# Memory keys with the contraction outermost, first loads on two queues, memory norm summed by slab, fewer stores, in a one-core decoder trunk

## The chip, the cores and the metric

The kernel runs on one core of one Trainium2 chip. The metric is the device time of one execution in microseconds, lower is better. All times below come from executions on the chip.

## The reference, cut to what matters

Two layers (`DEPTH = 2`) are run on a prompt of 256 tokens and on 8 samples of 4 tokens, with shared weights, `D_MODEL = 1024`, all in float32. Each layer begins with keys and values of 256 memory tokens; they depend on the memory input alone, so the kernel computes those of both layers before anything else. The trunk ends in one norm.

```python
def rmsnorm(x, g):
    xf = x.astype(F32)
    y = xf * lax.rsqrt(jnp.mean(xf * xf, axis=-1, keepdims=True) + EPS)
    return (y * g.astype(F32)).astype(x.dtype)
...
        mem_h = rmsnorm(mem_prompt, mem_norm[i])
        mk = (mem_h @ w_mem_k[i]).reshape(bp, n_mem, MEM_HEADS, MEM_HEAD_DIM)
        mv = (mem_h @ w_mem_v[i]).reshape(bp, n_mem, MEM_HEADS, MEM_HEAD_DIM)
        xp, npool, nconv, nssm = trunk_layer(
...
    y_prompt = rmsnorm(xp, final_norm)
    y_sample = rmsnorm(xs, final_norm)
```

## The kernel before

**Weights.** All weights are cut into tiles of 128 x 128 and packed in the order of use, eight to a slab of 512 KB. `Stream` runs them past TensorE. A slab is loaded by SyncE's queue into one of four `raw` buffers, then split into two float32r parts, `whi` on ScalarE (line 139) and `wlo = raw - whi` on VectorE (line 148). The first slab is loaded and split in two halves. Each product is three matmuls: high weight by high activation, high by low, low by high.

**Order of the work.** Every engine runs its instructions in program order. `take` hands out weight tiles; at the first tile of slab `s` it calls `tick(s)`, which issues loads up to slab `s+5`, then one stage of every generator that was given to `W.start(gen, delay)`, then the splits up to `whi(s+3)` and `wlo(s+2)`. A load into a `raw` buffer waits for the `wlo` that reads the buffer's last slab.

**The head.** The memory input `mem` lies transposed, contraction (1024) on partitions in eight chunks, two to a tile, 256 tokens wide. `mem_split` (from line 435) makes `memh` on ScalarE and `meml` on VectorE of a chunk. Slabs 0 to 3 are the keys of layer 0, 4 to 7 its values, 8 to 11 and 12 to 15 those of layer 1; the feed-forward starts at slab 16. In the keys one slab is one head: the eight chunks of the contraction go into one PSUM bank, then the next head starts. The values keep the contraction outermost already: a slab is two chunks, and two banks (`ps_v0`, `ps_v1`) take them.

The memory norm is applied behind the products. `mem_norm` squares the eight chunks on ScalarE, adds them into `macc` on GpSimd (`square`, line 297), sums columns with two small matmuls (`ps_mem`), takes the inverse root into `rv`, and spreads it over partitions with two more (`ps_rm`) into `Rm`. `mem_out` multiplies the key banks by `Rm` and stores them, `mem_out_v` the value banks by `rv`. `first_norm` prepares the first feed-forward's input chunk by chunk, and `load_x` loads it.

**The tail.** `Final.add` squares each of the eight chunks of `x` as the last down-projection delivers it and adds it into `facc` on GpSimd, the last chunk on VectorE. `Final.finish` sums columns (`ps_fin`), takes the inverse root, spreads it over partitions (`ps_spread`), copies that to `Rf`, and multiplies and stores each chunk by itself.

Of the kernel before, what the change touches and what calls it, by code (L numbers as in the profile page):

```python
# [20 lines left out]
NM = 256  # L21
# [23 lines left out]
def group_order(tiles, cuts):  # L45
    """Weight tiles (tile, k) of a group of products: all tiles up to each cut of k in turn."""
    for a, b in zip((0,) + cuts[:-1], cuts):
        for t in tiles:
            for k in range(a, b):
                yield t, k  # L50
# [41 lines left out]
def weight_plan():  # L92
    plan = []
    for i in range(L):
        for h in range(4):
            plan += [("w_mem_k", i, k * P, h * P) for k in range(KC)]
        for k in range(KC):
            plan += [("w_mem_v", i, k * P, c * P) for c in range(4)]
# [8 lines left out]
class Stream:  # L107
    """Runs the packed weight tiles past TensorE, each split into two float32r parts.

    Every SLAB tiles make a tick: the split of a later slab is issued, then one stage  # L110
    of every piece of side work that is under way."""
# [77 lines left out]
def trunk_kernel(ctx, tc, wpack, xT, memT, vecs, consts, wdt, wpool, hpool, hconv, h0T, kT, vC,  # L189
# [31 lines left out]
    def blocks(name):  # L221
        """Two tiles of zeros for block_fill()."""
# [5 lines left out]
    def block_fill(us, srcs, copy):  # L228
        """Block b of 32 columns, of each of the four slices, gets the slice's samples with all but sample b zero."""
# [60 lines left out]
    def products(tiles, cuts, xs):  # L290
        """One PSUM bank per tile: W[:, cols].T @ x."""
# [13 lines left out]
    def rstd_cols(accs, starts, width, name):  # L305
        """1 / sqrt(mean + eps) of the column sums of accs, tokens on partitions: [128, len(accs) * len(starts)]."""
# [16 lines left out]
    def rstd_rows(r, t, sums, width):  # L323
        """r = 1 / sqrt(sums / width + eps), elementwise; stages."""
# [11 lines left out]
    def spread(r):  # L336
        """out[p, t] = r of token t, for every partition p; r holds tokens 0.., 128.., 160.. by column."""
# [6 lines left out]
    class Norm:  # L344
        """Collects sum(x^2) chunk by chunk and splits x * gain for the products."""
# [23 lines left out]
    class Final:  # L369
        """The last norm: x * gain in place, then its scale and the output."""  # L370
# [4 lines left out]
        def add(self, c):  # L375
            xc = x[:, c, :]
            if c < KC - 1:
                square(self.acc, xc, c == 0)
            else:
                sq = tmp("sqr")  # L380
                tt(sq, xc, xc, ALU.mult)
                tt(self.acc, self.acc, sq, ALU.add)
            act(xc, xc, AF.Copy, scale=vec[:, V_FIN + c:V_FIN + c + 1])

        def add_lo(self, c):
            pass

        def finish(self):
            r = rstd_cols([self.acc], TOK, D, "fin")
            R = rp.tile([P, T], F32, tag="R", name="Rf")  # L390
            act(R, spread(r)[:, :T], AF.Copy)
            for c in (0, 5, 1, 2, 6, 3, 4, 7):
                tt(x[:, c, :], x[:, c, :], R, ALU.mult, G if c in (5, 6) else V)
                nc.sync.dma_start(out=o_y[:, c, :], in_=x[:, c, :])
# [17 lines left out]
    mem = [unit(f"mem{j}") for j in range(KC // 2)]  # L412

    def load_mem(j):
        nc.sync.dma_start(out=mem[j][:, :, :NM], in_=memT[:, 2 * j:2 * j + 2, :])

    gain0 = cp.tile([P, KC], F32, name="gain0")
    load_mem(0)
    nc.sync.dma_start(out=gain0, in_=vecs[:, V_MEM:V_MEM + KC])
    W.load_to(0)  # L420
    for j in range(1, KC // 2):
        load_mem(j)
    W.load_to(1)
    nc.sync.dma_start(out=vec, in_=vecs)
    W.load_to(2)
    nc.sync.dma_start(out=con, in_=consts)
    W.load_to(3)
# [18 lines left out]
    def mem_norm():  # L446
        for c in range(KC):
            square(macc, chunk(mem, c)[:, :NM], c == 0)
        yield
        yield  # L450
# [3 lines left out]
        yield  # L454
# [21 lines left out]
    def mem_out(i, kps, h, ksb):  # L476
        yield
# [11 lines left out]
    warm = rp.tile([P, 1], F32, tag="warm", name="warm", bufs=1)  # L489
    G.memset(warm, 0.0)  # L490
    act(warm, warm, AF.Copy)
    mem_split(0, range(2))
    W.split_to(0, 0)
    mem_split(0, range(2, KC))
    W.split_to(1, 1)
    W.start(mem_norm())
    W.start(load_x(), 1)
    n0 = Norm("n0", lambda c: col(0, V_F1, c))
    for i in range(L):
        mh, ml = mhl[i]  # L500
        ksb = k4.tile([P, 4, NM], F32, tag="k4", name="ksb")
        for h in range(4):
            ps = bank("ps_k")
            ws = [W.take() for k in range(KC)]
            for k in range(KC):
                mm(ps[:, :NM], ws[k][0], chunk(mh, k)[:, :NM], k == 0, False)
                mm(ps[:, :NM], ws[k][0], chunk(ml, k)[:, :NM], False, False)
            for k in range(KC):
                mm(ps[:, :NM], ws[k][1], chunk(mh, k)[:, :NM], False, k == KC - 1)
            W.start(mem_out(i, ps, h, ksb), max(0, 5 - h) if i == 0 else 0)  # L510
        if i == 0:
            W.start(first_norm(n0))
# [51 lines left out]
    def mixer(i, cur, nxt):  # L564
# [65 lines left out]
        def dt_work(ps_dt):  # L630
# [19 lines left out]
            # log1p(e) = 2 atanh(e / (2 + e))  # L650
# [13 lines left out]
            # cumulative sums, heads on partitions and tokens on partitions; sums to the end of the group  # L664
# [149 lines left out]
        def heads4(g):  # L814
            """Four heads of the prompt's scan: two pairs of heads, one group of B and C."""
# [170 lines left out]
        def softmax(ps, n):  # L986
            """Rows of ps [128, n, 256] (scores) to weights; stages."""
# [354 lines left out]
```

## Time and profile before

| | |
|---|---|
| median of 3 runs | 1600.78 us (1600.12 to 1602.69) |
| span of the profiled execution (first to last instruction) | 1597.1 us |
| that execution's own time | not recorded; the median is 3.7 us above the span |
| TensorE busy (PE, matmul) | 1558.0 us, 98% of the span |
| VectorE (DVE) / ScalarE (ACT) / GpSimd (POOL) busy | 67% / 50% / 19% |
| memory traffic over the span | 173 GB/s |
| chain that ended last, TensorE's share | 87% |

PE is TensorE's matmul row, PEld its weight loads, SPq the DMA issues of SyncE. Where a row says `[2.31 <-DVE meml L246]` the engine stood idle for 2.31 us before that instruction, and VectorE's writing of `meml` at line 246 ended it. The names before `<-` are outputs, those behind it inputs.

### The profile page before, as it was taken

To read this page: it belongs to the slowest core of one execution; us is meant where nothing else is said; L and a number is where in the kernel's file an instruction comes from. 1 tells how busy PE (TensorE), PEld (TensorE's weight loads), DVE (VectorE), ACT (ScalarE), POOL (GpSimd) and SP (SyncE) were. 2 spreads that over 40 slices of the span, in tenths; PEclk is the share of its full clock that TensorE was granted. 3 is DMA by queue.
4 is the path that set the end of the run, shared out by engine and by line. 5 is a ranking of instruction groups with operands and counts; after the bars stand their busy time and mean duration, and the time that the engine had idled before them with its cause. 6 is when DMAs were issued, how large, how long until landed. Compare 5 with 4: busy or idle time off the path is not lost.

```text
span 1597.1 us, 29305 instructions
## 1 busy us (share of the span) xinstructions
PE 1558.0 (98%) x11792; PEld 1502.7 (94%) x11792; DVE 1066.3 (67%) x1598; ACT 804.0 (50%) x1231; POOL 302.9 (19%) x368
## 2 busy tenths in 40 slices
PE   7999999988999999999999999999999999999997
PEld 6899999887889999999999999988888999999997
DVE  6765645788777867656456665588778786766643
ACT  7444434465565546444445444456557454644442
POOL 3000001368233102000000000046823320200001
PEclk9999999999999999999999999999999999999999
DMA  6744444546465454444444444554655545444452
GB/s 244 230 167 166 164 165 171 196 147 233 168 212 193 147 173 167 162 165 166 165 166 160 171 161 169 178 185 151 238 170 188 203 159 169 158 168 167 159 171 70
DMA packets 81287, 278.00 MB, mean 174 GB/s; under 512 B 9088, under 2 KB 14336, under 8 KB 81152
## 3 DMA queue, kind: packets, MB, share of 16 engines
q1 hardware_dynamic: 81152, 276.14, 50.2%
q8 instruction: 92, 1.51, 0.4%
q14 instruction: 43, 0.35, 0.1%
HBM read 262.39 MB, written 13.71 MB: 173 GB/s over the span
## 4 chain that ended last, share of the span: by engine, by line
PE 87%; DVE 8%; ACT 2%; DMA 1%; POOL 1%; issue 1%; SPq 0%; DVEq 0%; ACTq 0%; POOLq 0%
PE ps L249 61%; PE pd L249 18%; DVE cacc L246 4%; PE ps_y L249 2%; PE ps_v L249 1%; PE ps_k L249 1%; ACT L252 1%; DMA raw<-wpack 1%; PE ps_up L249 1%; DVE wlo L148 1%; DVE cbuf L237 1%; ACT cacc L252 1%; PE ps_yo L249 1%; ACT whi L139 1%; PE ps_sp L249 0%
## 5 line engine op out<-in xcount | busy, mean ns | idle before, releaser
L148 DVE TENSOR_TENSOR wlo<-raw,whi 128x1024 fp32r<-128x1024 f32 (+1 forms) x409 | 517.8, 1267 | 266.8 <-ACT hidh L252 99.9
L139 ACT ACTIVATE whi<-raw 128x1024 fp32r<-128x1024 f32 (+1 forms) x441 | 463.7, 1054 | 329.3 <-PE ps L249 153.2
L249 PE MATMUL ps<-n1h,whi 128*128 128x288 f32 x896 | 274.4, 306 | 5.4 <-DVE Bst L237 5.4
L249 PE MATMUL ps<-n1h,wlo 128*128 128x288 f32 x896 | 266.9, 298 | 4.8 <-POOL wlo L148 4.8
L249 PE MATMUL ps<-n1l,whi 128*128 128x288 f32 x896 | 266.3, 297 | 0.0
L249 PE MATMUL ps<-n2h,whi 128*128 128x288 f32 x704 | 208.8, 297 | 0.0
L249 PE MATMUL ps<-n0h,whi 128*128 128x288 f32 x704 | 208.6, 296 | 0.0
L249 PE MATMUL pd<-hidh,whi 128*128 128x288 f32 x704 | 208.4, 296 | 0.0
L249 PE MATMUL ps<-n0l,whi 128*128 128x288 f32 x704 | 207.7, 295 | 0.0
L249 PE MATMUL pd<-hidl,whi 128*128 128x288 f32 x704 | 207.7, 295 | 0.0
L249 PE MATMUL ps<-n2l,whi 128*128 128x288 f32 x704 | 207.7, 295 | 0.0
L249 PE MATMUL ps<-n2h,wlo 128*128 128x288 f32 x704 | 207.0, 294 | 0.0
L249 PE MATMUL ps<-n0h,wlo 128*128 128x288 f32 x704 | 207.0, 294 | 0.0
L249 PE MATMUL pd<-hidh,wlo 128*128 128x288 f32 x704 | 207.0, 294 | 0.0
L237 POOL TENSOR_TENSOR acc<-acc,sqr 128x288 f32<-128x288 f32 x42 | 44.7, 1064 | 786.9 <-ACT sqr L252 785.9
L249 PEld LDWEIGHTS ps<-n1h,whi 128*128 128x128 f32 x896 | 170.3, 190 | 16.1 <-DVE Bst L237 5.8
L249 PEld LDWEIGHTS ps<-n1h,wlo 128*128 128x128 f32 x896 | 170.4, 190 | 7.3 <-POOL wlo L148 6.9
L249 PEld LDWEIGHTS ps<-n1l,whi 128*128 128x128 f32 x896 | 170.5, 190 | 0.7
L249 PEld LDWEIGHTS ps<-n0h,wlo 128*128 128x128 f32 x704 | 132.6, 188 | 0.0
L249 PEld LDWEIGHTS pd<-hidh,wlo 128*128 128x128 f32 x704 | 132.6, 188 | 0.0
L249 PEld LDWEIGHTS ps<-n2h,wlo 128*128 128x128 f32 x704 | 132.6, 188 | 0.0
L249 PEld LDWEIGHTS ps<-n2l,whi 128*128 128x128 f32 x704 | 132.1, 188 | 0.1
(297 smaller groups left out, 2877.5 us busy)
## 6 DMA issues: line engine op xcount, KB each, us to landing
raw<-wpack SPq DMA_DIRECT2D x439, 512.0 KB, 3.3
kb<-kT SPq DMA_DIRECT2D x16, 512.0 KB, 5.1
vb<-vC SPq DMA_DIRECT2D x16, 512.0 KB, 4.6
hb<-h0T SPq DMA_DIRECT2D x16, 512.0 KB, 5.8
o_ssm_s<-hb SPq DMA_DIRECT2D x16, 512.0 KB, 5.0
x<-xT SPq DMA_DIRECT2D x4, 288.0 KB, 4.1
o_y<-x SPq DMA_DIRECT2D x8, 144.0 KB, 1.8
mem<-memT SPq DMA_DIRECT2D x4, 256.0 KB, 4.6
```

The lines of the kernel that those rows point to most:

```text
L139: nc.scalar.activation(out=hi[:, a], in_=self.loaded[self.n_hi][:, a], func=AF.Copy)
L148: eng.tensor_tensor(out=lo[:, a], in0=raw[:, a], in1=self.his[n][:, a].bitcast(F32), op=ALU.subtract)
L237: (eng or V).tensor_tensor(out=out, in0=a, in1=b, op=op)
L246: V.scalar_tensor_tensor(out=out, in0=a, scalar=s, in1=b, op0=op0, op1=op1)
L249: PE.matmul(out, lhsT=lhsT, rhs=rhs, start=start, stop=stop)
L252: A.activation(out=out, in_=a, func=func, **kw)
```

## The change

Keys: the packed order of `w_mem_k` becomes that of `w_mem_v`, so a key slab is two chunks of the contraction for all four heads, and four PSUM banks are filled side by side. Loads: `mem` 0 and the gain go to ScalarE's queue; on SyncE's the two halves of slab 0 come first, then `mem` 1, slab 1, `mem` 2 and 3, slab 2, `vec`, slab 3, `con`. Splits: `meml`/`memh` of chunks 4 to 7 come after the split of slab 1. Memory norm: the seven additions go from GpSimd to VectorE, and the eight squares are put into two ticks (1 and 2) in place of one (0). The start of `load_x` is 2 ticks later, that of `first_norm` 3 ticks. Two matmuls on a tile of zeros (`still`) are put ahead of everything on TensorE; nothing reads their result.

Tail: the last chunk's square is no longer added into `facc`; its column sums are taken by themselves and added at [128, 3]. A dummy square root stands behind chunk 5. The chunks are multiplied straight from the PSUM bank on VectorE (six) and from `Rf` on GpSimd (two), and stored by five DMAs, three of them for two chunks.

```diff
@@ def weight_plan():
-        for h in range(4):
-            plan += [("w_mem_k", i, k * P, h * P) for k in range(KC)]
-        for k in range(KC):
-            plan += [("w_mem_v", i, k * P, c * P) for c in range(4)]
+        for name in ("w_mem_k", "w_mem_v"):
+            for k in range(KC):
+                plan += [(name, i, k * P, c * P) for c in range(4)]
@@ class Final
-                sq = tmp("sqr")
-                tt(sq, xc, xc, ALU.mult)
-                tt(self.acc, self.acc, sq, ALU.add)
+                self.sq = tmp("sqr")
+                tt(self.sq, xc, xc, ALU.mult)
             act(xc, xc, AF.Copy, scale=vec[:, V_FIN + c:V_FIN + c + 1])
+            if c == KC - 3:
+                act(warm, warm, AF.Sqrt)
...
+        def sums(self, acc):
+            ps = bank("ps_fin")
+            for j, s in enumerate(TOK):
+                mm(ps[:, j:j + 1], acc[:, s:s + P], ones[:, 0:1])
+            return ps
+
         def finish(self):
-            r = rstd_cols([self.acc], TOK, D, "fin")
+            v, r = (sp.tile([P, 3], F32, tag=f"fin{k}", name=f"fin{k}") for k in range(2))
+            ts(v, self.sums(self.acc)[:, :3], 1.0 / D, ALU.mult, EPS, ALU.add)
+            stt(v, self.sums(self.sq)[:, :3], 1.0 / D, v, ALU.mult, ALU.add)
+            act(r, v, AF.Sqrt)
...
+            ps = spread(r)
             R = rp.tile([P, T], F32, tag="R", name="Rf")
-            act(R, spread(r)[:, :T], AF.Copy)
-            for c in (0, 5, 1, 2, 6, 3, 4, 7):
-                tt(x[:, c, :], x[:, c, :], R, ALU.mult, G if c in (5, 6) else V)
-                nc.sync.dma_start(out=o_y[:, c, :], in_=x[:, c, :])
+            act(R, ps[:, :T], AF.Copy)
+            for c, n in ((0, 0), (6, 0), (1, 2), (2, 0), (3, 2), (7, 2), (4, 1), (5, 1)):
+                if c < 6:
+                    tt(x[:, c, :], ps[:, :T], x[:, c, :], ALU.mult)
+                else:
+                    tt(x[:, c, :], x[:, c, :], R, ALU.mult, G)
+                if n:
+                    nc.sync.dma_start(out=o_y[:, c + 1 - n:c + 1, :], in_=x[:, c + 1 - n:c + 1, :])
@@ first loads
-    load_mem(0)
-    nc.sync.dma_start(out=gain0, in_=vecs[:, V_MEM:V_MEM + KC])
+    load_mem(0, A)
+    A.dma_start(out=gain0, in_=vecs[:, V_MEM:V_MEM + KC])
     W.load_to(0)
-    for j in range(1, KC // 2):
-        load_mem(j)
+    load_mem(1, nc.sync)
     W.load_to(1)
+    for j in range(2, KC // 2):
+        load_mem(j, nc.sync)
+    W.load_to(2)
     nc.sync.dma_start(out=vec, in_=vecs)
-    W.load_to(2)
+    W.load_to(3)
     nc.sync.dma_start(out=con, in_=consts)
-    W.load_to(3)
@@ def mem_norm():
-            square(macc, chunk(mem, c)[:, :NM], c == 0)
-        yield
-        yield
+            src = chunk(mem, c)[:, :NM]
+            if c == 0:
+                act(macc, src, AF.Square)
+            else:
+                sq = tmp("sqr", NM)
+                act(sq, src, AF.Square)
+                tt(macc, macc, sq, ALU.add)
+            if c % 4 == 3:
+                yield
         yield
         r = rstd_cols([macc], (0, P), D, "mem")
@@ head
+    still = wide("still")
+    V.memset(still, 0.0)
...
+    ps = bank("ps_still")
+    for j in range(2):
+        mm(ps, still[:, :P], still)
     mem_split(0, range(2))
     W.split_to(0, 0)
-    mem_split(0, range(2, KC))
+    mem_split(0, range(2, 4))
     W.split_to(1, 1)
-    W.start(mem_norm())
-    W.start(load_x(), 1)
+    mem_split(0, range(4, KC))
+    W.start(mem_norm(), 1)
+    W.start(load_x(), 3)
...
+        pss = [bank("ps_k") for h in range(4)]
+        for k in range(KC):
+            ws = [W.take() for h in range(4)]
+            for part, xs in ((0, mh), (0, ml), (1, mh)):
+                for h in range(4):
+                    mm(pss[h][:, :NM], ws[h][part], chunk(xs, k)[:, :NM], k == 0 and part == 0 and xs is mh,
+                       k == KC - 1 and part == 1)
         for h in range(4):
-            ps = bank("ps_k")
-            ws = [W.take() for k in range(KC)]
-            for k in range(KC):
-                mm(ps[:, :NM], ws[k][0], chunk(mh, k)[:, :NM], k == 0, False)
-                mm(ps[:, :NM], ws[k][0], chunk(ml, k)[:, :NM], False, False)
-            for k in range(KC):
-                mm(ps[:, :NM], ws[k][1], chunk(mh, k)[:, :NM], False, k == KC - 1)
-            W.start(mem_out(i, ps, h, ksb), max(0, 5 - h) if i == 0 else 0)
+            W.start(mem_out(i, pss[h], h, ksb), 1 if i == 0 else 0)
         if i == 0:
-            W.start(first_norm(n0))
+            W.start(first_norm(n0), 3)
```

How the instructions stand is told by three places. The first is TensorE at the start of layer 0's keys. Before, from the end of the first head into the second (`memh0` holds chunks 0 and 1, `memh3` chunks 6 and 7):

```order
L249 MATMUL ps_k_167<-memh3_125,whi_134 128x256
L249 MATMUL ps_k_167<-meml3_129,whi_134 128x256
L249 MATMUL ps_k_167<-memh0_122,wlo_137 128x256 x2
L249 MATMUL ps_k_167<-memh1_123,wlo_137 128x256 x2
L249 MATMUL ps_k_167<-memh2_124,wlo_137 128x256 x2
L249 MATMUL ps_k_167<-memh3_125,wlo_137 128x256 x2
L249 MATMUL ps_k_224<-memh0_122,whi_152 128x256
L249 MATMUL ps_k_224<-meml0_126,whi_152 128x256
```

Of the change, TensorE's first key matmuls (`whi_139` is slab 0):

```order
L248 MATMUL ps_k_172<-memh0_127,whi_139 128x256
L248 MATMUL ps_k_173<-memh0_127,whi_139 128x256
L248 MATMUL ps_k_174<-memh0_127,whi_139 128x256
L248 MATMUL ps_k_175<-memh0_127,whi_139 128x256
L248 MATMUL ps_k_172<-meml0_131,whi_139 128x256
L248 MATMUL ps_k_173<-meml0_131,whi_139 128x256
L248 MATMUL ps_k_174<-meml0_131,whi_139 128x256
L248 MATMUL ps_k_175<-meml0_131,whi_139 128x256
L248 MATMUL ps_k_172<-memh0_127,wlo_142 128x256
```

Before, the first slab uses all eight memory chunks and its low part comes last; now it uses chunks 0 and 1 alone, and its low part from the ninth matmul on.

The second place is VectorE between the memory splits and the norm's root. Before (`wlo_154` is slab 1, `wlo_230` slab 3, `wlo_262` slab 4):

```order
L246 SCALAR_TENSOR_TENSOR meml3_129<-mem3_96,gain0_97,memh3_125 128x256 x2
L148 TENSOR_TENSOR wlo_154<-raw_106,whi_152 128x1024
L148 TENSOR_TENSOR wlo_198<-raw_109,whi_194 128x1024
L148 TENSOR_TENSOR wlo_230<-raw_112,whi_196 128x1024
L148 TENSOR_TENSOR wlo_262<-raw_168,whi_228 128x1024
L243 TENSOR_SCALAR rs_v_294<-ps_mem_291 128x2
```

Of the change (`wlo_184` is slab 2, `wlo_224` slab 3, `wlo_266` and `wlo_297` slabs 4 and 5):

```order
L245 SCALAR_TENSOR_TENSOR meml3_134<-mem3_96,gain0_97,memh3_130 128x256 x2
L147 TENSOR_TENSOR wlo_184<-raw_108,whi_180 128x1024
L236 TENSOR_TENSOR macc_118<-macc_118,sqr_213 128x256
L236 TENSOR_TENSOR macc_118<-macc_118,sqr_216 128x256
L236 TENSOR_TENSOR macc_118<-macc_118,sqr_219 128x256
L147 TENSOR_TENSOR wlo_224<-raw_111,whi_182 128x1024
L236 TENSOR_TENSOR macc_118<-macc_118,sqr_252 128x256
L236 TENSOR_TENSOR macc_118<-macc_118,sqr_255 128x256
L236 TENSOR_TENSOR macc_118<-macc_118,sqr_258 128x256
L236 TENSOR_TENSOR macc_118<-macc_118,sqr_261 128x256
L147 TENSOR_TENSOR wlo_266<-raw_176,whi_222 128x1024
L147 TENSOR_TENSOR wlo_297<-raw_178,whi_264 128x1024
```

The seven additions into `macc` now stand on VectorE, three ahead of slab 3's low part and four ahead of slab 4's.

The third place is VectorE behind the last chunk's square, to the end. Before:

```order
L237 TENSOR_TENSOR sqr<-x 128x288
L237 TENSOR_TENSOR facc<-facc,sqr 128x288
L243 TENSOR_SCALAR rs_v<-ps_fin 128x3
L317 RECIPROCAL rs_r<-rs_r 128x3
L246 SCALAR_TENSOR_TENSOR rs_v<-rs_v,rs_r 128x3
L237 TENSOR_TENSOR rs_v<-rs_v,rs_r 128x3
L246 SCALAR_TENSOR_TENSOR rs_r<-rs_v,rs_r 128x3
L237 TENSOR_TENSOR x<-x,Rf 128x288 x6
```

Of the change:

```order
L236 TENSOR_TENSOR sqr<-x 128x288
L242 TENSOR_SCALAR fin_17868<-ps_fin 128x3
L245 SCALAR_TENSOR_TENSOR fin_17868<-ps_fin,fin_17868 128x3
L399 RECIPROCAL fin_17869<-fin_17869 128x3
L245 SCALAR_TENSOR_TENSOR fin_17868<-fin_17868,fin_17869 128x3
L236 TENSOR_TENSOR fin_17868<-fin_17868,fin_17869 128x3
L245 SCALAR_TENSOR_TENSOR fin_17869<-fin_17868,fin_17869 128x3
L236 TENSOR_TENSOR x<-ps_spread,x 128x288 x6
```

The 128 x 288 addition is gone, one operation at 128 x 3 is new, and the six products read the PSUM bank in place of `Rf`.

## Rows read from the trace of the kernel before

**Rows 1.** The page, busy time and share of the span by engine.

```profile
PE 1558.0 (98%) x11792; PEld 1502.7 (94%) x11792; DVE 1066.3 (67%) x1598; ACT 804.0 (50%) x1231; POOL 302.9 (19%) x368
```

**Rows 2.** TensorE's waits, whole run: total us, times, longest us.

```profile
PE ps_mem L249 <- POOL macc L237: 2.5, 1, 2.5
PE ps_k L249 <- DVE meml L246: 2.3, 1, 2.3
```

**Rows 3.** Busy time, granted clock and traffic by stretch, us from the start.

```profile
core 0: us, PE busy (x) PEld busy (x) DVE busy (x) ACT busy (x) POOL busy (x), PEclk, DMA share, GB/s
0.00:5.76 5.76, 0.00 (x1) 0.00 (x1) 0.91 (x3) 3.02 (x5) 0.30 (x5) 1.00 0.58 184
5.76:10.84 5.08, 4.67 (x14) 3.44 (x15) 3.90 (x8) 3.36 (x8) 0.00 (x0) 1.00 0.91 307
10.84:14.26 3.42, 3.42 (x22) 3.42 (x23) 1.34 (x2) 3.42 (x10) 1.60 (x2) 1.00 1.04 423
21.36:26.01 4.65, 4.65 (x29) 4.65 (x29) 2.54 (x8) 3.33 (x7) 0.00 (x0) 0.69 0.82 265
63.62:1584.93 1521.31, 1503.66 (x11482) 1454.61 (x11481) 1015.73 (x1521) 762.67 (x1159) 286.01 (x347) 1.00 0.50 172
1584.93:1597.10 12.17, 1.68 (x12) 1.49 (x12) 5.69 (x14) 2.43 (x4) 2.03 (x2) 0.70 0.27 97
```

**Rows 4.** Timeline of the start: start us, duration us, instruction, idle before.

```profile
0.74 0.44 SPq L415 DMA_DIRECT2D mem<-memT  x1
1.74 0.90 SPq L130 DMA_DIRECT2D raw<-wpack  x2
3.68 0.91 ACT L252 ACTIVATE memh<-mem,gain 128x256 fp32r<-128x256 f32 x2 [1.45 <-DMA gain<-vecs]
...
5.08 1.38 ACT L139 ACTIVATE whi<-raw 128x512 fp32r<-128x512 f32 x2 [0.49 <-DMA raw<-wpack]
...
5.76 0.58 PE L249 MATMUL ps_k<-memh,whi 128*128 128x256 f32 x1 [5.76 <-ACT whi L139]
...
10.84 1.06 ACT L139 ACTIVATE whi<-raw 128x1024 fp32r<-128x1024 f32 x1 [0.40 <-DMA raw<-wpack]
```

**Rows 5.** Timeline, TensorE: eight key matmuls back to back, twice.

```profile
14.94 1.11 PE L249 MATMUL ps_k<-memh,wlo 128*128 128x256 f32 x8
...
24.30 1.91 PE L249 MATMUL ps_k<-memh,wlo 128*128 128x256 f32 x8
```

**Rows 6.** The chain that ended last: start us, us, what.

```profile
54.80 0.48 PE ps_norm L249 x2
55.28 8.33 PE ps_v L249 x36
```

**Rows 7.** Timeline of the memory norm, and one VectorE split.

```profile
12.11 2.25 ACT L252 ACTIVATE sqr<-mem 128x256 f32<-128x256 f32 x7
12.59 8.72 POOL L237 TENSOR_TENSOR macc<-macc,sqr 128x256 f32<-128x256 f32 x7 [11.75 <-ACT sqr L252]
...
23.30 1.22 DVE L148 TENSOR_TENSOR wlo<-raw,whi 128x1024 fp32r<-128x1024 f32 x1
```

**Rows 8.** Timeline of the tail.

```profile
1586.01 0.46 DVE L237 TENSOR_TENSOR facc<-facc,sqr 128x288 f32<-128x288 f32 x1
1586.49 1.28 ACT L252 ACT_TABLE_LOAD   x1
1586.52 0.83 PE L249 MATMUL ps_fin<-con,facc 128*128 128x1 f32 x6 [1.61 <-DVE facc L237]
...
1587.79 0.20 ACT L252 ACTIVATE rs_r<-rs_v 128x3 f32<-128x3 f32 x1
...
1589.73 0.41 ACT L252 ACTIVATE Rf<-ps_spread 128x288 f32<-128x288 f32 x1 [1.74 <-PE ps_spread L249]
1590.17 3.49 DVE L237 TENSOR_TENSOR x<-x,Rf 128x288 f32<-128x288 f32 x6 [1.39 <-ACT Rf L252]
...
1590.66 4.23 SPq L394 DMA_DIRECT2D o_y<-x  x8
```

More of the change, by code (lines that the diff above doesn't have):

```diff
@@ L379, in add @@
             else:
-                sq = tmp("sqr")
-                tt(sq, xc, xc, ALU.mult)
-                tt(self.acc, self.acc, sq, ALU.add)
+                self.sq = tmp("sqr")
+                tt(self.sq, xc, xc, ALU.mult)
             act(xc, xc, AF.Copy, scale=vec[:, V_FIN + c:V_FIN + c + 1])
+            if c == KC - 3:
+                act(warm, warm, AF.Sqrt)
         def add_lo(self, c):
             pass
-        def finish(self):
-            r = rstd_cols([self.acc], TOK, D, "fin")
-            R = rp.tile([P, T], F32, tag="R", name="Rf")
-            act(R, spread(r)[:, :T], AF.Copy)
-            for c in (0, 5, 1, 2, 6, 3, 4, 7):
-                tt(x[:, c, :], x[:, c, :], R, ALU.mult, G if c in (5, 6) else V)
-                nc.sync.dma_start(out=o_y[:, c, :], in_=x[:, c, :])
+        def sums(self, acc):
[3 more added lines that the diff above has]
+            return ps
+        def finish(self):
+            v, r = (sp.tile([P, 3], F32, tag=f"fin{k}", name=f"fin{k}") for k in range(2))
+            ts(v, self.sums(self.acc)[:, :3], 1.0 / D, ALU.mult, EPS, ALU.add)
+            stt(v, self.sums(self.sq)[:, :3], 1.0 / D, v, ALU.mult, ALU.add)
+            act(r, v, AF.Sqrt)
+            V.reciprocal(out=r, in_=r)
+            stt(v, v, -0.5, r, ALU.mult, ALU.mult)
+            tt(v, v, r, ALU.mult)
+            stt(r, v, 1.5, r, ALU.add, ALU.mult)
+            ps = spread(r)
+            R = rp.tile([P, T], F32, tag="R", name="Rf")
+            act(R, ps[:, :T], AF.Copy)
[6 more added lines that the diff above has]
+                    nc.sync.dma_start(out=o_y[:, c + 1 - n:c + 1, :], in_=x[:, c + 1 - n:c + 1, :])
             yield
@@ L412, in trunk_kernel, with load_mem @@
     mem = [unit(f"mem{j}") for j in range(KC // 2)]
-    def load_mem(j):
-        nc.sync.dma_start(out=mem[j][:, :, :NM], in_=memT[:, 2 * j:2 * j + 2, :])
+    def load_mem(j, eng):
+        eng.dma_start(out=mem[j][:, :, :NM], in_=memT[:, 2 * j:2 * j + 2, :])
     gain0 = cp.tile([P, KC], F32, name="gain0")
-    load_mem(0)
-    nc.sync.dma_start(out=gain0, in_=vecs[:, V_MEM:V_MEM + KC])
+    load_mem(0, A)
+    A.dma_start(out=gain0, in_=vecs[:, V_MEM:V_MEM + KC])
     W.load_to(0)
-    for j in range(1, KC // 2):
-        load_mem(j)
+    load_mem(1, nc.sync)
     W.load_to(1)
+    for j in range(2, KC // 2):
+        load_mem(j, nc.sync)
+    W.load_to(2)
     nc.sync.dma_start(out=vec, in_=vecs)
-    W.load_to(2)
+    W.load_to(3)
     nc.sync.dma_start(out=con, in_=consts)
-    W.load_to(3)
     Rm = tmp("Rm", NM)
@@ L453, in mem_norm @@
         V.tensor_copy(out=rv, in_=r)
-        yield
         yield
@@ L476, in mem_out @@
     def mem_out(i, kps, h, ksb):
-        yield
         tt(ksb[:, h, :], kps[:, :NM], Rm, ALU.mult)
```

## The prediction

> **What bounds the kernel now.** I read the page first: TensorE is busy 98% of the span [rows 1]. Then the stretches: from 63.62 to 1584.93 us, where the feed-forwards and mixers run, it is busy 1503.66 of 1521.31 us at full granted clock [rows 3]. The change touches nothing there, so I take those 1521.3 us as they are. What is left is the head up to 63.62 us and the tail of 12.17 us [rows 3]. The sum is a sum of shifts: how much earlier the first feed-forward starts, and how much shorter the tail is.
>
> In the head the reader should see four losses. TensorE starts at 5.76 us, when the first half of slab 0 is split [rows 4]. It first runs slowly: eight key matmuls take 1.91 us at the lower of the two clock levels (1.2 GHz) and 1.11 us at the upper (2.4 GHz), which the granted clock of 0.69 over 21.36 to 26.01 shows as a mixture [rows 3, 5]. It waits 2.5 us for the sum of squares, which GpSimd adds up for 8.72 us, and 2.3 us for `meml` of layer 1 [rows 2, 7]. The values of layer 0 start at 26.01 us, the edge of a stretch [rows 3].
>
> **The change part by part, head.** A key matmul has 256 columns, 0.213 us each at 1.2 GHz; eight of them and an overhang of 0.2 behind the last make the slow row's 1.91. Read the same way, the fast row gives (1.11 - 0.17) / 8 = 0.118 us each [rows 5]. So a slab of 24 is 2.8 us fast, 5.1 slow; the four key slabs 11.3 or 20.4. A value slab of 12 is 8.33/3 = 2.8 us fast [rows 6].
>
> *First product.* ScalarE waited for the gain until 3.68, then split `mem` 0 (0.91), then waited for slab 0's half until 5.08 [rows 4]. The change issues the slab's first half at the front of its own queue, one 0.44 us issue and the gain's sooner [rows 4], so that wait of 0.49 can go. Against it: `mem` 0 now shares the DMA engines with slab 0. Bounds: 5.3 us (the 0.49 saved) and 6.8 us (`mem` 0 usable only when slab 0's first half was, 5.08, then 0.91 and two half splits of 0.69); I take 6.0, nearer to the middle since neither row shows two queues.
>
> *Data.* Up to 5.76 us 184 GB/s moved 1.06 MB, up to 10.84 another 307 x 5.08 = 1.56 MB, then 423 GB/s [rows 3]. Before, slab 1 was the 2.10th MB in the queue's order; by these rates it had moved at 9.15, and it was usable at 10.84 [rows 4], a lag of 1.7 us. In the new order slab 1 is complete at 1.57 MB (usable 9.1), slab 2 at 2.62 MB (12.5), slab 3 at 3.34 MB with `vec` (14.2). This is the point of the reordering: a key slab now needs only its own two chunks, so TensorE can follow the loads.
>
> *Splits and slab 3.* ScalarE splits slab 3 from 14.2 to 15.3 (1.06 each, [rows 4]); then four squares at 0.32 (2.25/7, [rows 7]) end at 16.6. VectorE has three additions into `macc` queued ahead of slab 3's low part. I price one at 0.46, the same addition at 288 columns [rows 8]; the first starts when the second square is there (16.0), so they end at 17.4, and `wlo` of slab 3 (1.22, [rows 7]) at 18.6. That is the added wait: behind these additions stand VectorE's splits, and TensorE waits for them. On TensorE slabs 0 to 2 are through by about 16 at the fast rate; of slab 3 the eight high products can go, the other 16 (1.9 us) wait for 18.6 and end at 20.5. The column sums `ps_mem` cost some 0.6 (two columns; three took 0.83 at the end [rows 8]). **The values start at 21.1 in place of 26.0: 4.9 us.** The wait on GpSimd goes with it: the last four additions end at 18.6 + 4 x 0.46 = 20.4, before TensorE asks. If the additions cost nothing, slab 3 ends at 19 and the values start at 19.6; if TensorE is slow through slabs 0 and 1 (to 16.2) it costs nothing more, since slab 3 waits anyway; slow through slab 2 it costs 1 to 2 us.
>
> *The zero matmuls* are two of 512 columns in float32. `ps_norm`, the same kind at 288 columns, took 0.48 [rows 6], so each is 0.85 us fast or 1.7 slow, 3.4 together; begun near 1.3 us they end before 5. They cost nothing while the first product is later than that; without this cover they cost up to 3.4. What they bring is a clock that may have risen earlier, which slab 3's wait hides.
>
> A rule of the Trainium skill, page "TensorE: Matmul & The Clock Gate", section "Part 1: The HAM clock gate", says that the clock is throttled by default, that activity releases it, and that the monitor does not restart with the kernel, so the number of slow matmuls varies from run to run. No row here shows work ahead of 5.76 us, so it can't be held against the trace; if the rise came only after slab 2, the values would start 1 to 2 us later, which is a rival below.
>
> *From the values to the feed-forward* it was 63.62 - 26.01 = 37.6 us. The wait of 2.3 us for `meml` [rows 2] came since VectorE had to make all eight chunks of layer 1 before the first head was done; now two chunks are needed per slab, and `first_norm` with its GpSimd additions begins three ticks later. I take the whole 2.3 as gone, bounds 0 and 2.5. What is late next is `rv`: slabs 4 and 5's low parts stand ahead of it on VectorE (20.4 + 2 x 1.22 = 22.8), then a root and five small operations, each near the 0.20 of the tail's root [rows 8], 1.2 in all: 24.0, and `ps_rm` is asked for at 21.1 + 2.8 = 23.9. I add 0.2, bounds 0 and 1.5. **Feed-forward at 21.1 + 37.6 - 2.3 + 0.2 = 56.6 us in place of 63.62: 7.0 us.** `first_norm` ends three ticks (some 8 us) later against the feed-forward; its result is wanted four slabs into it, some 11 us or more, so this is hidden by those products; uncovered it would cost the part over 8.
>
> A second rule, page "DMA: Bandwidth & Descriptors", section "Queues, rings and completion order": each DMA engine takes turns between the queues it has work for, packet by packet. No run here shows two queues. By it `mem` 0, in pieces half as long as slab 0's, would land only with slab 0's second half, and the first product would come near the 6.8 of my bounds; slab 3's wait hides that in the sum.
>
> **The tail.** Gone from the path: the addition into `facc`, 0.46, with its hand-over 0.55; the table load's excess, since the root started at 1587.79 although `ps_fin` ended at 1587.35 and its scaling is a small operation of some 0.2, so 0.2; the copy `Rf`, 0.44 from 1589.73 to 1590.17 [rows 8]. New: one 128 x 3 operation is the same length as the one it replaces on the path. So the products start 1.2 us earlier. They last 3.49 us now, with eight stores issued over 4.23 [rows 8]; the last issue begins some 0.8 us after the last product. Five issues need 5 x 0.45 = 2.2 us, so the last store follows its product at once: 0.8 more at best, 0.2 at worst if two-chunk stores land later or the products from PSUM are slower. **Tail: 1.4 to 2.1, taken as 1.9.** The dummy root puts 1.3 us on ScalarE some 15 us before the end; there it is busy 50% [rows 1], so it is hidden.
>
> **Sum.** 7.0 + 1.9 = 8.9 us. The span becomes 1588.2 from 1597.1; the median of the runs is 3.7 above the span and I leave that difference: 1600.8 - 8.9 = **1591.9 us**. Differences of up to 0.2% (3.2 us) can hardly be told from no change here.
>
> **Rivals.**
> - *Follows the loads.* The additions don't hold slab 3 (squares earlier or VectorE faster): values at 19.6, `ps_rm` without a wait: 1.7 us better, 1590.2; with the tail at 2.1 and faster loads 1588.5. For it: VectorE's idle time between slabs. Against: program order.
> - *The head gives back.* VectorE takes splits, `meml`, `ksb` and `macc` in less time than before and again is late in layer 1's keys: the 2.3 us stay and `ps_rm` waits 1.2: 1591.9 + 3.3 = 1595.2.
> - *Clock late.* All four key slabs slow: 6.0 + 20.4 + 0.9 = 27.3 for the values, 6.2 later than forecast: 1598.1; slow through slab 2 only: 1593.5. For it: before, the rows from 5.76 on are slow for about 7 us, with gaps. Against: now the engine has fewer gaps when slow.
> - *Slower.* The same clock mechanism, kept low through the values of layer 0 as well, because the load-paced keys leave gaps: 48 value matmuls at twice 0.23 add 11 us to the 1598.1: 1609. It decides once the slow stretch costs over 8.9 + 3.2 = 12.1 us, that is the keys and half of the values. Against: at 24.30 the engine was slow and by 54.80 at full rate [rows 5, 6], and dense value matmuls leave no gaps.
> - *The head doesn't do what it says:* the feed-forward is bound by the raw stream. Up to slab 16 some 13 MB must come; at 423 GB/s [rows 3] that is 31 us, so there is room. If it were so only the tail stays: 1598.9.
>
> **How the numbers follow.** Forecast 0.53 (own range 1590 to 1594), follows the loads 0.20, gives back 0.12, clock late 0.10 (half of it near 1593.5), head without gain 0.02, slower 0.03. Range for 8 in 10: 1587.0, the better rival's 1588.5 less the spread of runs, to 1596.5, which takes in the rival that gives back and the bounds of `ps_rm` and the tail. Faster by over 0.2% (below 1597.6): the first three and half of the fourth, 0.90; within: the other half and the fifth, 0.07; slower: 0.03.
>
> **What would show each step.** Values' first matmul at 20 to 22 us; feed-forward's near 56; `wlo` of slab 3 directly behind three additions on VectorE, and TensorE's wait ahead of slab 3 ended by it; no wait on GpSimd for `ps_mem`; no wait of over 1 us in layer 1's keys; no table load in the tail, the products starting about 4.0 us after the last down matmul in place of 5.2; last store issued at once behind its product. Wrong if slow key matmuls reach past slab 2, if TensorE waits for `rv`, `meml` or a `raw` load beyond 22 us, or if the stretch between feed-forward and tail is not 1521 us long.

## The result, and the profile after

The changed kernel took 1588.65 us, median of four runs (1587.69 to 1590.54), beside 1600.72 us for the kernel before on the same chip: a ratio of 0.9922 (95% interval 0.9908 to 0.9936). Run again later beside other kernels it took 1589.72 (five runs, 0.9928, 0.9914 to 0.9941). Forecast were 1591.9 us, so the gain of 8.9 us came out as 11 to 12. Both times lie below the forecast's own range of 1590 to 1594 and inside the range for 8 in 10. In every run whose span is known, of either kernel, the time is about 1.8 us above the span of that run. So the profiled run of before took about 1598.9 us, at the low end of its kernel's times, and that is the rest of the 3.7 us that the prediction carried along: 1.9 of the 3.2 us between the forecast and the first median come from it.

The changed kernel was profiled twice, here and in the later batch; the second profile is named as such. The stretches of the first (us, engines with count, granted clock, DMA share, GB/s), which answer to [rows 3]:

```profile
0.00:5.52 5.52, 3.78 (x4) 1.17 (x4) 0.48 (x1) 1.49 (x2) 0.30 (x5) 1.00 0.63 189
5.52:8.26 2.74, 1.18 (x5) 1.18 (x6) 2.08 (x4) 2.65 (x7) 0.00 (x0) 1.00 1.01 341
8.26:10.87 2.61, 2.61 (x17) 2.61 (x16) 2.43 (x6) 2.61 (x6) 0.00 (x0) 1.00 1.06 407
10.87:12.64 1.77, 1.77 (x18) 1.77 (x16) 1.77 (x5) 1.07 (x3) 0.00 (x0) 1.00 1.03 412
55.18:1575.18 1520.00, 1502.80 (x11485) 1453.94 (x11484) 1017.08 (x1524) 764.09 (x1162) 286.07 (x347) 1.00 0.51 172
1575.18:1585.90 10.72, 2.23 (x17) 1.95 (x17) 4.08 (x14) 1.15 (x3) 1.55 (x2) 0.75 0.29 111
```

One column has to be read with care. The granted clock is recorded as 1.00 from the start, also in 5.76 to 10.84 of [rows 3], yet up to 10.5 us four key matmuls here take 1.05 us. That is their length at a recorded clock of 0.50 in the second profile; later four take 0.64. For the first microseconds the level is therefore inferred from durations.

The start, against [rows 4]: ScalarE waits for the gain until 5.61 us (3.68 before), the first key matmul comes at 7.08 (5.76 before), and slab 1, usable at 10.84 before, is split from 8.26.

```profile
5.61 0.91 ACT L251 ACTIVATE memh<-mem,gain 128x256 fp32r<-128x256 f32 x2 [2.37 <-DMA gain<-vecs]
6.42 1.13 ACT L138 ACTIVATE whi<-raw 128x512 fp32r<-128x512 f32 x2
...
7.08 1.22 PE L248 MATMUL ps_k<-memh,whi 128*128 128x256 f32 x4 [1.85 <-ACT whi L138]
...
8.26 1.04 ACT L138 ACTIVATE whi<-raw 128x1024 fp32r<-128x1024 f32 x1
```

The chain that ended last (start us, us, what), against [rows 6]. From 7.08 us to the feed-forward it is TensorE alone, and neither wait of [rows 2] is left:

```profile
7.08 13.09 PE ps_k L248 x96
20.18 0.34 PE ps_mem L248 x4
20.51 2.91 PE ps_v L248 x12
23.42 0.44 PE ps_rm L248 x4
23.87 8.34 PE ps_v L248 x36
32.20 11.41 PE ps_k L248 x96
43.62 11.08 PE ps_v L248 x48
54.69 0.48 PE ps_norm L248 x2
```

The tail, against [rows 8]. No table load stands in it; the products start at 1579.66, 4.5 us after the last down matmul, behind the copy `Rf` and not behind `ps_spread`:

```profile
1576.21 0.83 PE L248 MATMUL ps_fin<-con,sqr 128*128 128x1 f32 x6 [0.48 <-DVE sqr L236]
...
1577.27 0.20 ACT L251 ACTIVATE fin<-fin 128x3 f32<-128x3 f32 x1 [0.55 <-DVE fin L245]
...
1578.33 0.85 PE L248 MATMUL ps_spread<-con,fin 128*128 128x128 f32 x6 [1.29 <-DVE fin L245]
1579.22 0.41 ACT L251 ACTIVATE Rf<-ps_spread 128x288 f32<-128x288 f32 x1 [1.74 <-PE ps_spread L248]
1579.66 2.28 DVE L236 TENSOR_TENSOR x<-ps_spread,x 128x288 f32<-128x288 f32 x6 [1.39 <-ACT Rf L251]
...
1580.51 2.57 SPq L412 DMA_DIRECT2D o_y<-x  x5
```

By stages:

| us | before | forecast | after | second profile |
|---|---|---|---|---|
| first key matmul | 5.76 | 6.0 | 7.08 | 7.11 |
| values of layer 0 | 26.01 | 21.1 | 20.51 | 20.65 |
| feed-forward | 63.62 | 56.6 | 55.18 | 55.31 |
| feed-forward to last down matmul | 1521.3 | 1521.3 | 1520.0 | 1521.5 |
| tail | 12.17 | 10.3 | 10.72 | 11.37 |
| span | 1597.1 | 1588.2 | 1585.9 | 1588.2 |

What was expected of the second profile:

> The changed kernel once more, for a second look at the clock of the keys and a time beside the other runs of this call: median 1588 to 1589.5, first key matmul near 7.1 us, slow until somewhere between 10.3 and 12.8, values at 20.3 to 21.9, no wait of TensorE over 0.2 us from there to the feed-forward, first product of the tail 4.45 after the last down matmul.

Its span is the forecast's, but by a different sum: a better head and a worse tail. Runs of one kernel beside each other differ by up to 3.3 us, so effects below 2 us are read from the stages.

### The profile page after: what moved, and what is told of

It is laid out like the page before. It is cut to its first block, busy times and chain, and to the rows that moved or that the text cites. A ratio compares the mean times of both kernels' runs of the same rounds, so it can differ in the third digit from the quotient of the medians.

```text
span 1585.9 us, 29321 instructions
## 1 busy us (share of the span) xinstructions
PE 1556.9 (98%) x11802; PEld 1500.9 (95%) x11802; DVE 1063.2 (67%) x1606; ACT 803.7 (51%) x1232; POOL 296.5 (19%) x361
## 4 chain that ended last, share of the span: by engine, by line
PE 89%; DVE 7%; ACT 2%; POOL 1%; issue 0%; DMA 0%; ACTq 0%; DVEq 0%
PE ps L248 62%; PE pd L248 18%; DVE cacc L245 4%; PE ps_y L248 2%; PE ps_k L248 2%; PE ps_v L248 1%; PE ps_up L248 1%; ACT L251 1%; PE ps_yo L248 1%; ACT cacc L251 1%; DVE cbuf L236 1%; PE ps_sp L248 0%; PE ps_pv L248 0%; PE ps_row L248 0%; DVE z L236 0%
## 5 line engine op out<-in xcount | busy, mean ns | idle before, releaser
L248 PEld LDWEIGHTS ps<-n0l,whi 128*128 128x128 f32 x704 | 132.2, 188 | 0.1
```

What stands on the lines that cost most here:

```text
L248: PE.matmul(out, lhsT=lhsT, rhs=rhs, start=start, stop=stop)
```

## The experiments

**The zero matmuls.** Theory A: they bring a fast clock to the keys. B: slab 3's wait hides what they bring.

```diff
-    for j in range(2):
-        mm(ps, still[:, :P], still)
```

> The changed kernel without the two matmuls on zeros and their memset. Theory of the prediction (the zero matmuls bring nothing that shows, since TensorE waits for slab 3 anyway): first key matmul still near 7.1 us, values start at most 0.3 us later than the 20.5 of the changed kernel, 1588.7 to 1589.0 us. Rival (in the changed kernel TensorE never waits between 7.1 and 55.2 us, so its clock sets the pace): slow key matmuls for some 5 to 7 us in place of 3.3, values start at 21.5 to 23.5, time 1590 to 1592.

Measured 1590.38 us; the key stage in the chain:

```profile
7.21 14.27 PE ps_k L248 x96
```

It is 1.2 us longer than in the first profile, since key matmuls ran at the lower level until 12.8 and not 10.5 us, and no wait absorbed it; the feed-forward came at 56.48. That the missing zero matmuls are the cause is not shown. One of the four runs took 1587.84 us, as little as the best of the changed kernel. And a kernel below that has them (`load_x` at its old tick) shows the same stage, with the lower level until 12.7:

```profile
7.17 14.31 PE ps_k L248 x96
```

In the second profile, with them too, the keys ran fast for 1.5 us, then at a granted clock of 0.50, the lower level:

```profile
7.11:8.66 1.55, 1.55 (x13) 1.55 (x14) 1.55 (x3) 1.43 (x4) 0.00 (x0) 0.99 1.09 401
8.66:12.06 3.40, 3.40 (x18) 3.40 (x17) 2.98 (x7) 3.30 (x6) 0.00 (x0) 0.50 1.04 404
```

**One queue.** `mem` 0 and the gain back on SyncE's queue.

```diff
-    load_mem(0, A)
-    A.dma_start(out=gain0, in_=vecs[:, V_MEM:V_MEM + KC])
+    load_mem(0, nc.sync)
+    nc.sync.dma_start(out=gain0, in_=vecs[:, V_MEM:V_MEM + KC])
```

> The changed kernel with mem 0 and the gain on SyncE's queue again, ahead of slab 0; all other loads in the new order. Theory A (on two queues mem 0 and the gain share the DMA engines with slab 0 and land late): gain usable near 3.7 us in place of 5.5, first key matmul near 5.8 in place of 7.1, values 0.8 to 1.3 us earlier, 1587.4 to 1587.9. Theory B (what mem 0 gains, slab 0 and the slabs behind it lose by 0.9 us of later issue): first key matmul 5.8, but TensorE waits for slab 1 or 2 and the values start at 20.5 as now, 1588.7.

Measured 1590.13 us, nearer to B. TensorE's timeline:

```profile
5.84 0.74 PE L248 MATMUL ps_k<-memh,whi 128*128 128x256 f32 x4 [0.61 <-ACT whi L138]
...
9.62 0.74 PE L248 MATMUL ps_k<-memh,whi 128*128 128x256 f32 x4 [0.65 <-ACT whi L138]
...
18.20 0.74 PE L248 MATMUL ps_k<-memh,wlo 128*128 128x256 f32 x4 [0.68 <-DVE wlo L147]
...
21.26 0.50 PE L248 MATMUL ps_v<-wlo,memh 128*128 128x512 f32 x1 [0.19 <-DVE wlo L147]
```

The first product comes 1.2 us earlier and is fast at once (four in 0.74 us, not 1.22), and all of that is lost again: to slab 1, then to the low part of slab 3, which stands behind the additions as the prediction said. Feed-forward at 55.84.

**More zero matmuls** separate the clock from the loads: four fill the time up to the first key matmul.

```diff
-    for j in range(2):
+    for j in range(4):
```

> The changed kernel with four zero matmuls in place of two. At the two durations read so far they would end near 6.9 us, just ahead of the first key matmul (7.1). A (the zero matmuls helped little because TensorE stood still for 1.9 us behind them; with a gap of 0.6 us the keys were fast at once): the first key matmul runs at about 7.1 to 7.3 and is fast at once or within 1 us; the first products then run into the low part of slab 3 (16.96 in the changed kernel), values at 19.2 to 19.8, feed-forward at 53.9 to 54.5, about 1 us less than the changed kernel in the stage table. B (the clock rises by its own schedule): slow key matmuls until 10.3 to 12.8 as before, values at 20.5 to 21.9, feed-forward at 55.2 to 56.5. C (the zero matmuls themselves stay slow): they end at 8.6 and hold the first key matmul back to 8.7, values at 20.5 to 21.

Measured 1588.9 us (0.9929, 0.9915 to 0.9944). The keys are fast from 7.19 on, and the same wait appears:

```profile
17.57 0.75 PE L248 MATMUL ps_k<-memh,wlo 128*128 128x256 f32 x4 [0.58 <-DVE wlo L147]
...
20.63 0.50 PE L248 MATMUL ps_v<-wlo,memh 128*128 128x512 f32 x1 [0.19 <-DVE wlo L147]
```

A is right on the clock and wrong on its worth: feed-forward at 55.20, as in the changed kernel (55.18, 55.31). Keys that are slow for 3.3 us or a wait for VectorE: two limits that lie within some tenths of each other. Keys that are slow for 5.5 us cost 1.3 more (56.48 above).

**The sum on GpSimd**, as before, the rest new.

```diff
-                tt(macc, macc, sq, ALU.add)
+                tt(macc, macc, sq, ALU.add, G)
```

> The changed kernel with the seven additions into macc on GpSimd, in the same two ticks. Theory A (GpSimd's 1.19 us for one addition sets ps_mem): seven of them from about 14 us end at 22 to 23, TensorE waits 2 to 3 us ahead of ps_mem, time 1590.7 to 1592.5. Theory B (with the squares spread over two ticks the place of the sum doesn't matter): no wait, values at 20.5 or earlier since VectorE is relieved of 3.5 us, 1588.4 to 1588.9.

Measured 1591.54 us. TensorE waits again, though for less than the 2.5 of [rows 2]; the feed-forward starts at 58.07, 2.9 later, of which the slow clock (until 12.7) is a part:

```profile
22.82 0.61 PE L248 MATMUL ps_mem<-con,macc 128*128 128x1 f32 x4 [1.32 <-POOL macc L236]
```

**The keys by head**: the old order, the rest new.

```diff
-        for name in ("w_mem_k", "w_mem_v"):
-            for k in range(KC):
-                plan += [(name, i, k * P, c * P) for c in range(4)]
+        for h in range(4):
+            plan += [("w_mem_k", i, k * P, h * P) for k in range(KC)]
...
```

> The changed kernel with the keys' old order: head by head, all eight chunks for the first slab. A (the order lets TensorE follow the loads): the first slab's matmuls on chunks 4 to 7 wait for memh 4 to 7, which in the changed kernel's trace come some 4 us after the first key matmul, so the values of layer 0 start at 21.5 to 23 us in place of 20.5; in layer 1 the first slab again needs all chunks of meml and TensorE waits for them, up to the 2.3 us of before; feed-forward at 56.5 to 59.5 in place of 55.2, time 1590 to 1593. B (the loads, the sum and the zero matmuls do it alone, and the order of the keys nothing): values at 20.5 to 21, no wait in layer 1, feed-forward at 55 to 55.7, 1588.7.

Measured 1593.78 us (0.996, 0.9945 to 0.9975). First TensorE's timeline, then the chain:

```profile
11.35 0.58 PE L249 MATMUL ps_k<-meml,whi 128*128 128x256 f32 x1 [0.68 <-DVE meml L246]
```

```profile
11.35 13.10 PE ps_k L249 x87
24.45 0.34 PE ps_mem L249 x4
24.79 2.90 PE ps_v L249 x12
```

Up to 11.35 us TensorE gets nine matmuls done, in pieces, and stays slow until 17.2. Undoing the order costs 4.1 us at the feed-forward (59.30), the slow clock included. But layer 1 has no wait here: A was wrong in that part.

**The keys alone**, on the kernel before; the edit is the reverse of the last one.

> The kernel before with the new order of the keys alone; loads, sum, ticks and tail are the old ones. A (the order takes the wait for meml of layer 1 away, and the rest of the gain in the head is from loads and sum): ps_mem still waits for GpSimd's additions until about 21.3 us, values at 25 to 26 as before, no wait of over 1 us in layer 1's keys, feed-forward at 61 to 61.5 in place of 63.6, 1598.3. B (VectorE is late in layer 1 for its own load, whatever the order): the wait of about 2.3 us stays, feed-forward at 63.5, 1600.7. C (the order is worth most of the head's gain): values at 22 or earlier, feed-forward at 57 or earlier, 1594 or less.

Measured 1597.48 us (0.9982, 0.9973 to 0.9992). TensorE's timeline:

```profile
21.93 0.61 PE L248 MATMUL ps_mem<-con,macc 128*128 128x1 f32 x4 [2.58 <-POOL macc L236]
...
45.75 0.74 PE L248 MATMUL ps_k<-memh,wlo 128*128 128x256 f32 x4 [0.18 <-DVE wlo L147]
```

A holds: the wait in layer 1 shrinks from 2.31 to 0.18, the one on GpSimd stays, and the feed-forward starts at 62.37. Together with the last run: either the order or the rest of the change takes the 2.3 us away. In layer 0 the order brings nothing here, since TensorE still waits for GpSimd.

**`load_x` and `first_norm` at their old ticks.**

```diff
-    W.start(load_x(), 3)
+    W.start(load_x(), 1)
...
-            W.start(first_norm(n0), 3)
+            W.start(first_norm(n0))
```

> The changed kernel with load_x and first_norm started at their old ticks (1 and 0 in place of 3 and 3). Theory A (the order of the keys removed the wait of 2.3 us for meml): no wait of over 0.3 us in layer 1's keys, feed-forward at 55 to 55.5 us, 1588.7. Theory B (the later start of first_norm removed it by relieving VectorE): a wait of 1 to 2.3 us in layer 0's values or layer 1's keys, feed-forward at 56 to 57.5, 1589.7 to 1591.

Measured 1590.17 us. No wait in layer 1 either, as A has it; the 1.3 us at the feed-forward (56.52) are those of keys that were slow until 12.7.

**The gain ahead of `mem` 0** on ScalarE's queue: the two lines that issue them change places.

> The changed kernel with the gain (4 KB) issued ahead of mem 0 on ScalarE's queue. A (the gain was late because its packets stood behind mem 0's, which share the DMA engines with the other queue): the gain is usable before 4.5 us, first key matmul at 6.2 to 6.8 in place of 7.1, the still time behind the two zero matmuls 1.0 to 1.6 us in place of 1.9; if the clock then holds, values at 19.6 to 20.6 with a wait on the low part of slab 3, else at 20.5 to 21. B (mem 0 itself is as late as the gain, since two transfers on the second queue take what they take): first key matmul 7.0 to 7.2, nothing changes.

Measured 1589.26 us. The first key matmul comes at 6.63, half a microsecond earlier, because now `mem` 0 is the one that lands last, at 5.1; then slow keys and 0.4 of waits for VectorE, feed-forward at 55.65. In this profile the order on the queue is a third of the 1.2 us that one queue brought. But it didn't repeat: the last kernel below has the same order, `mem` 0 comes at 5.58 and the first key matmul at 7.05, as in the changed kernel.

```profile
5.58 0.91 ACT L251 ACTIVATE memh<-mem,gain 128x256 fp32r<-128x256 f32 x2 [2.42 <-DMA mem<-memT]
```

So what the order is worth stays open; in both profiles the second queue was slower than one queue (5.84).

**The copy behind the first product.**

```diff
-            act(R, ps[:, :T], AF.Copy)
...
                     tt(x[:, c, :], ps[:, :T], x[:, c, :], ALU.mult)
+                    if c == 0:
+                        act(R, ps[:, :T], AF.Copy)
```

> The changed kernel with the copy Rf on ScalarE written behind the first product of the tail in place of ahead of it. A (the copy kept VectorE off the bank of ps_spread, and only one engine at a time reads it): the first product starts at once behind the spread, 0.45 us earlier, 4.05 us after the last down matmul in place of 4.5; the copy then waits for that product and the second product for the copy, so the other products and the end of the span stay within 0.1 of the changed kernel, tail 10.7. B (the wait had another cause, such as VectorE's own chain): first product 4.5 after the last down matmul as before.

The tail of this kernel:

```profile
1581.05 0.46 DVE L236 TENSOR_TENSOR x<-ps_spread,x 128x288 f32<-128x288 f32 x1 [0.95 <-PE ps_spread L248]
1581.54 0.41 ACT L251 ACTIVATE Rf<-ps_spread 128x288 f32<-128x288 f32 x1 [2.23 <-DVE x L236]
1581.98 1.92 DVE L236 TENSOR_TENSOR x<-ps_spread,x 128x288 f32<-128x288 f32 x5 [0.48 <-ACT Rf L251]
```

A: the first product starts 4.05 us after the last down matmul, the copy waits for it, the second product for the copy. In these programs two engines read this bank one after the other, by their waits; the tail stays 10.8. Time 1590.34 (two runs).

**Two tries for a better kernel.** The first takes VectorE's additions away: four zero matmuls, four chunks summed on GpSimd, four by TensorE, a second spread bank for the copy.

```diff
+                for a, acc in enumerate(accs):
+                    mm(ps[:, j:j + 1], acc[:, s:s + P], ones[:, 0:1], a == 0, a == len(accs) - 1)
...
+            act(R, spread(r)[:, :T], AF.Copy)
...
+                tt(sq, src, src, ALU.mult, G)
+                tt(macc, macc, sq, ALU.add, G)
...
```

> The changed kernel with four zero matmuls; the squares of chunks 0 to 3 made and added up on GpSimd, those of chunks 4 to 7 made on ScalarE and summed by TensorE itself (ps_mem over five sources), so that VectorE has no addition into macc; in the tail two spread banks, one for VectorE's seven products and one for the copy, and four stores of two chunks. A (with a fast clock VectorE's additions set the start of the values): low part of slab 3 done near 15.5 us, no wait of TensorE on wlo, ps_mem about 0.85 in place of 0.34, values at 19.3 to 19.8 where the kernel with four zero matmuls alone had 20.3 to 20.6, feed-forward at 53.8 to 54.3; tail: first product about 4.05 after the last down matmul, 10.2 in place of 10.7; about 1.4 us below the changed kernel in the stage table, time near 1587.3. B (the loads set it): a wait on raw or whi of slab 3 or 4 takes the place of the one on wlo, values at 20.2 or later, only the tail's 0.45 is left. C (GpSimd's eight operations slow VectorE or come late): wait on POOL macc ahead of ps_mem, values at 21 or later.

Measured 1591.36 us, slower than the changed kernel. VectorE and GpSimd, TensorE, and the chain:

```profile
8.82 1.71 DVE L245 SCALAR_TENSOR_TENSOR meml<-mem,gain,memh 128x256 fp32r<-128x256 f32 x2
10.46 1.76 DVE L147 TENSOR_TENSOR wlo<-raw,whi 128x1024 fp32r<-128x1024 f32 x1
```

```profile
8.43 1.07 POOL L236 TENSOR_TENSOR macc<-macc,sqg 128x256 f32<-128x256 f32 x1
...
10.33 0.80 POOL L236 TENSOR_TENSOR macc<-macc,sqg 128x256 f32<-128x256 f32 x1
```

```profile
12.27 0.74 PE L248 MATMUL ps_k<-memh,wlo 128*128 128x256 f32 x4 [0.99 <-DVE wlo L147]
```

```profile
12.27 7.87 PE ps_k L248 x64
20.14 2.12 PE ps_mem L248 x20
22.26 4.46 PE ps_v L248 x12
```

C, in a place I had not named: while GpSimd works, two `meml` take 1.71 us in place of 0.88 and a `wlo` 1.76 in place of 1.22, and TensorE waits 0.99 us for it in slab 1. The keys are fast on both sides of that wait. The larger loss comes behind them: the column sums, twenty matmuls of one column for the changed kernel's four, take 2.12 us for 0.34, and the first values 4.46 for 2.91, at a granted clock of 0.62. The feed-forward starts at 58.48. The Trainium skill, page "SBUF — State Buffer", section "SBUF: two separate sides", has VectorE and GpSimd share one port pair that one of them holds while the other is blocked; the longer VectorE rows agree.

The second keeps GpSimd out: gain first, three zero matmuls, VectorE's three additions behind the low part of slab 3, the other four chunks summed by TensorE, and in the tail four matmuls on the identity ahead of `ps_spread`.

```diff
+            keep = bank("ps_keep")
+            for j in range(4):
+                mm(keep[:, :P], ident, ident)
...
+        for sq in sqs[1:]:
+            tt(macc, macc, sq, ALU.add)
...
```

> The changed kernel with: gain ahead of mem 0; three zero matmuls; VectorE's three additions into macc behind the low part of slab 3 and no others, the squares of chunks 4 to 7 summed by TensorE (ps_mem over five sources), nothing on GpSimd; in the tail four small matmuls on the identity while TensorE would stand still ahead of ps_spread, two spread banks, four stores of two chunks. A (VectorE's order sets the values once the clock is fast): first key matmul 6.6 to 6.9 and fast at once, no wait on wlo of slab 3 over 0.2, values at 19.0 to 19.8, feed-forward at 53.5 to 54.3 (changed kernel 55.2 and 55.3); tail: ps_spread's first bank 0.85 and not 1.5, first product 4.05 after the last down matmul, tail 10.1 to 10.3 (changed kernel 10.7 and 11.4); together 1.4 to 2.2 below the changed kernel by stages, time 1586.5 to 1588. B (the loads set it, which differ by 1.2 us from run to run): TensorE waits for whi or wlo of slabs 1 to 3 in other places by as much, values at 20.3 or later, only the tail's gain is left, time 1588 to 1589.

Measured 1591.67 us. The head does what A says up to 18.89 us, 1.3 earlier than the changed kernel, with no wait. Then the chain has

```profile
18.89 2.12 PE ps_mem L248 x20
21.01 4.46 PE ps_v L248 x12
```

the same loss as in the first try; I had put the twenty matmuls at 0.85 us. The stretches show that the values are slow by the clock, granted at 0.62 although TensorE never stood still:

```profile
18.89:21.01 2.12, 2.12 (x20) 2.12 (x21) 1.22 (x1) 2.10 (x3) 0.00 (x0) 1.00 0.74 245
21.01:25.47 4.46, 4.46 (x15) 3.53 (x15) 2.90 (x9) 2.13 (x5) 0.00 (x0) 0.62 0.88 304
```

In the tail the products start at 1583.08, 4.03 us after the last down matmul, as forecast for the change itself. The span still ends 11.05 us after that matmul: the longest of its stores took 3.2 us from issue to landing, where those of the first try, in the same order, took at most 2.4. The kernel with this order and the old four-matmul sum was not tried. Nor were the tail's other parts (the last square by itself, the dummy root, the merged stores) undone one by one; what they bring is read from the rows alone.

## Why the prediction came out as it did

*First product: wrong.* 7.08 and 7.11 us lie outside 5.3 to 6.8. The step bounded the late case by `mem` 0, which was there at 4.6; the gain, 4 KB behind it on the same queue, took 4.3 us from issue to landing where it had taken 2.4. One queue gives 5.84, gain first 6.63 in one kernel and 7.05 in another. The bound of 6.8 is also not what its terms add up to: 5.08, 0.91 and one half split of 0.69 are 6.7, with two 7.4. The rule of the Trainium skill, page "DMA: Bandwidth & Descriptors", section "Queues, rings and completion order" (turns packet by packet), had given 6.8 by way of `mem` 0; 7.08 lies nearer to that than to my 6.0, but the late transfer was the gain, and no row shows the turns themselves.

*Data: too slow.* Slabs 1, 2 and 3 were split from 8.26, 10.87 and 12.64 (second profile 8.50, 11.25, 13.08), forecast 9.1, 12.5 and 14.2. I had carried one load's lag of 1.7 us and the early 307 GB/s over; the stretches show 341 and then 407. This is the term that was mis-sized most, by 1.1 to 1.6 us at slab 3.

*Slab 3 behind the additions: right as a mechanism, not what ended first.* The low part was done at 16.96 (second profile 17.41) for 18.6, and TensorE, late and slow, came to it later. Where the clock is fast (one queue, four zero matmuls) the wait is there, 0.58 to 0.68 us. So the values began at 20.51 for 21.1. The price of an addition, 0.50 for 0.46, was right; that of the column sums, 0.34 for 0.6, too high.

*The zero matmuls "bring nothing that shows": not refuted, but the reason failed.* No wait at slab 3 hid anything in the changed kernel. With two of them the keys ran slowly for 3.3 to 3.5 us in three profiles and for 5.4 to 5.5 in two, without them for 5.6 in one, so the 1.2 us between those cases can't be put down to them. With a clock that is fast at once nothing more was gained. The Trainium skill, page "TensorE: Matmul & The Clock Gate", section "Part 1: The HAM clock gate", lets the number of slow matmuls vary from run to run; the two profiles of one kernel agree (fast for good from 10.5 and from 12.1 us).

*Values to feed-forward: right.* 34.67 us for a forecast 35.5: the 2.3 went, `ps_rm` waited for nothing, and of the rest 0.2 is the edge I had read as 26.01 (the chain of before has the first value matmul at 26.21); the last 0.4 were not followed. But the reason was too narrow: the order is enough for it, and so is the rest of the change.

*Tail: one step failed.* 1.45 us gained for 1.9 in the first profile. The addition and the table load left the path as said; the copy did not, since the copy and VectorE's first product read one bank and the program lets the copy go first: 0.44 us. The second profile gained 0.80 alone, since `ps_spread` took 1.49 us there, at a granted clock of 0.50, and 0.85 in the first, at 1.00:

```profile
1579.98 1.49 PE L248 MATMUL ps_spread<-con,fin 128*128 128x128 f32 x6 [1.29 <-DVE fin L245]
```

*Body: right.* 1520.0 and 1521.5 for 1521.3; what the first profile has less is no part of the change.

The three head terms that were off, first product +1.1, data -1.6 at slab 3 and values to feed-forward -0.8, do not add up, since TensorE follows whichever is last; the sum was 1.4 us too late at the feed-forward. That it came so near is in part luck: the first product and the data were off in opposite directions. Of the rivals, "follows the loads" has the time that came (1588.5 to 1590.2), but its cause, additions that hold nothing, is true only while TensorE is slow. That the time fell into its range also owes 1.9 us to the difference between median and span that was carried along.

## What to carry to other kernels

Cut the first products so that each needs only the loads that have come, and do not count on a second queue to bring the first one's transfers sooner: here the first product came 1.2 us later with it. Where two limits lie close together, taking away one shows the other; a fast clock or an earlier start was worth nothing while VectorE's order stayed as it was. Before moving reads of one PSUM bank to two engines, look at who waits for whom in the order.

## What was not expected of the hardware

- Behind two zero matmuls TensorE stood still for 1.85 to 2.19 us in six profiles of five kernels. In two profiles the key matmuls were fast for 1.3 to 1.5 us and then slow, at a granted clock of 0.50; in the other four they were slow at once, and whether the clock had risen before the pause is not shown. After 0.61 us (one queue) they stayed fast, after 1.39 (gain first) they were slow, after 1.33 (the last kernel, with three zero matmuls) fast.
- Twenty matmuls of one column in 2.1 us, with no pause, were followed by a granted clock of 0.62 in both kernels that had them; four in 0.34 us were not.
- In the tail `ps_spread` took 0.85 us in six profiles (before among them) and 1.5 in seven, behind a pause of 1.3 to 1.5 us; the granted clock was 1.00 in all of the six and 0.50 in all of the seven. With small matmuls in the pause, in the one kernel that had them, it took 0.87 at 1.00.
- The loads came at different paces in runs of like kernels: slab 3 was split from 12.64 to 13.79 us.
